# Other places for the opening loads, and the third pair of up-projection features split, summed and halved in another way

## The chip, the cores and the metric

The kernel runs on one core of one Trainium2 chip. The metric is the device time of one execution in microseconds (us); smaller is better. The core has a matrix engine (TensorE: PE in the profile, its weight loads PEld), VectorE (DVE), ScalarE (ACT), GpSimd (POOL) and SyncE (SP), which here issues the DMAs. All engines run their own instruction stream in order and wait for each other by semaphores.

## The reference, cut to what matters

One layer of an encoder for 1024 prompt rows and 64 sample rows of 1024 values. All is float32.

```python
z = einsum('btd,de->bte', x, w_in)            # one projection; columns: q_f k_f v_f f_lg u_g v_g q_s k_s v_s
log_f = log_sigmoid(f_lg + b_f)               # forget gates: 6 columns
o_f = fox_block(q_f, c, k_f, v_f)             # c = cumsum(log_f); softmax attention with forgetting
o_s = sb_block(q_s, k_s, v_s)                 # stick-breaking attention
o_g = sgu_mix(u, v, w_s, b_s)                 # spatial gating in chunks of 128
mix = rmsnorm_per_head(concat(o_f, o_g, o_s)) * g_mix @ w_out
x1 = layer_norm(ALPHA * x + mix)
y  = layer_norm(ALPHA * x1 + square(relu(x1 @ w_up)) @ w_down)
```

`w_up` has 4096 columns, here called features.

## The kernel before, in words

**Precision.** TensorE multiplies a fast 32-bit format (fp32r). So each operand is split into a high part (a ScalarE copy into fp32r) and a low part (`lo_sub`, L98: source minus high part, on VectorE or GpSimd), and each product is three matmuls: high by high, high by low, low by high (`PASSES`, a pair being the part of the rows and the part of the weights).

**Opening.** Row tile t of x (128 rows by 1024) is loaded by `x_load` (L312), transposed on TensorE in eight 128 by 128 blocks (`xtp`, L321) and split into `xT`. The weights of the first head pair stand in one tile `wkvfox` with 262 columns: 128 of K, 128 of V and 6 of the forget gates. `load_w` loads such columns in two groups g of four 128-row blocks each (`raw`, L337), ScalarE makes the high part (L338), and the low part is made on GpSimd for g = 0 and on VectorE for g = 1 (for the gates on GpSimd both). `load_kv` (L888) calls it for K, then loads row tile 1, then V, then the gates. A row tile's product with these weights is `kvfox` (L362), 24 matmuls per tile, group 0 of the weights first. Tiles of x are `row` buffers (seven places); K's raw weights have two `raw` places.

**Order.** Most of the program is written as generators whose steps are interleaved, and a scheduler with a model of time then fixes each engine's order. A change in one place can so move instructions far behind it. Two stretches are kept by `in_order`: every engine there runs as the code is written.

**Mix.** The output projection per row tile (`mx`, L251) takes the transposed heads `oTb`; LayerNorm of a tile, its store, and the transposes for the next tile and for the up-projection (`x_steps`) run between.

**Up-projection.** `w_up` is taken in 16 pairs of 128 features (p = 0 to 15), by a fast product scheme of seven half-size products instead of eight (`PROD`): operands 0, 1 and 3 are blocks of the weights, held in `wa[:, 0]`, `wa[:, 1]`, `wa[:, 2]`; operands 2, 4, 5 and 6 are sums of blocks, held in `ws`. Product 0 takes operand 0, product 1 operand 1, product 2 operand 5, product 3 operand 4. Each product is 12 matmuls for each of two groups of tokens (`Chain` s = 0 of 288 columns and s = 1 of 256). `prep(p)` splits the three blocks (`split` L1232: high on ScalarE, low on GpSimd), then `summed` makes the four sums in place in the raw tile `wr` (`w_sums`, L1241 to L1245, VectorE), `high` copies them to fp32r (L1514, ScalarE, in two halves) and `low` subtracts (VectorE, one instruction of 2048 columns). The first two sums overwrite the feature block f1, the last two f0; so the first waits for the split that reads f1's second half (operand 3), which is the third of the three. For p = 2 this stands inside the stretch kept by `in_order`, between the products of p = 1; from p = 2 on TensorE takes each product for both token groups.

**Down-projection.** It follows in the same manner; it isn't touched.

Of the kernel before, what the change touches and what calls it, by code (L numbers as in the profile page):

```python
# [12 lines left out]
F32 = mybir.dt.float32  # L13
# [7 lines left out]
P = 128  # L21
PASSES = ((0, 0), (0, 1), (1, 0))
D = 1024
# [14 lines left out]
OFF_QF, OFF_KF, OFF_VF, OFF_FL = 0, 384, 768, 1152  # L38
# [4 lines left out]
ROWS = 7  # L43
# [13 lines left out]
def _build(nc, tc, a, es):  # L57
    def trows(t):
        return P if t < NB else TS
# [7 lines left out]
    w_in = a["w_in"].rearrange("l d e -> (l d) e").rearrange("(k p) e -> p k e", p=P)  # L67
# [7 lines left out]
    def xrows(t):  # L75
        return x_p[t * P:(t + 1) * P, :] if t < NB else x_s
# [20 lines left out]
    def lo_sub(eng, out, src, hi):  # L97
        eng.tensor_tensor(out, src, hi.bitcast(F32), op=ALU.subtract)  # L98
# [187 lines left out]
    sp = p12.enter_context(tc.tile_pool(name="sp", bufs=1, side="left"))  # L286
# [3 lines left out]
    with ExitStack() as p1:  # L290
# [16 lines left out]

        xT = [big.tile([P, 4, 2 * TT], F32R, name=f"xT{i}", tag="xw") for i in range(2)]

        def x_load(t):  # L310
            xr = sp.tile([P, D], F32, name=f"xr{t}", tag="row", bufs=ROWS)
            nc.sync.dma_start(xr[0:trows(t), :], xrows(t))  # L312
            return xr

# [12 lines left out]
        def xh(k, h, c0, n):  # L327
            return xT[k // 4][:, k % 4, h * LO + c0:h * LO + c0 + n]

        def load_w(dst, c0, col, n, tag="raw", dve=()):  # L330
            for g in range(2):
                hi = dst[:, 4 * g:4 * g + 4, 0, c0:c0 + n]
                lo = dst[:, 4 * g:4 * g + 4, 1, c0:c0 + n]
                rt = sp.tile([P, 4, P if n == P else n], F32, name=f"raw{col}_{g}", tag=tag,
                             bufs={"raw": 2, "row": ROWS, "ft": 4}[tag])
                raw = rt[:, :, 0:n]
                nc.sync.dma_start(raw, w_in[:, 4 * g:4 * g + 4, col:col + n])  # L337
                nc.scalar.activation(hi, raw, AF.Copy)  # L338
                lo_sub(nc.vector if g in dve else nc.gpsimd, lo, raw, hi)

# [536 lines left out]
        for fox, hp in ((True, 2), (True, 1), (True, 0), (False, 0), (False, 1), (False, 2)):  # L877
            first = not pairs
# [4 lines left out]
                off=(OFF_QF, OFF_KF, OFF_VF) if fox else (OFF_QS, OFF_KS, OFF_VS),  # L883
# [4 lines left out]
        def load_kv(st):  # L888
            dve = (1,) if st["quick"] else ()
            w = st["wkv"] = sp.tile([P, KT, 2, 262], F32R, name=f"wkv{st['nm']}", tag="wkv", bufs=1)  # L890
            load_w(w, 0, st["off"][1] + st["hp"] * P, P, dve=dve)
            if st["first"]:
                xrs[1] = x_load(1)
                load_w(w, P, st["off"][2] + st["hp"] * P, P, "row", dve=dve)
                load_w(w, 2 * P, OFF_FL, 6, "ft")
            else:
                load_w(w, P, st["off"][2] + st["hp"] * P, P, dve=dve)

# [176 lines left out]
        xrs = {}  # L1075
# [18 lines left out]
        while f_live or a_live:  # L1094
# [11 lines left out]
            if go_a:  # L1106
# [5 lines left out]
                try:  # L1112
                    c = next(A)
# [8 lines left out]
            elif f_live:  # L1122
                try:
                    c = next(F)
# [27 lines left out]
    xr = rp.tile([P, 4096], F32, name="xr", tag="ws")  # L1152
# [78 lines left out]
    def split(hi, lo, raw, eng):  # L1231
        nc.scalar.activation(hi, raw, AF.Copy)  # L1232
        lo_sub(eng, lo, raw, hi)


    def w_sums(f0, f1, part=(0, 1)):

        a, b = slice(0, 4), slice(4, 8)
        tt = nc.vector.tensor_tensor
        if 0 in part:  # L1240
            tt(f1[:, b], f1[:, a], f1[:, b], op=ALU.add)  # L1241
            tt(f1[:, a], f0[:, a], f1[:, a], op=ALU.subtract)
        if 1 in part:
            tt(f0[:, a], f1[:, b], f0[:, a], op=ALU.subtract)  # L1244
            tt(f0[:, b], f0[:, b], f0[:, a], op=ALU.subtract)  # L1245
# [100 lines left out]
    for i in range(MIXED, NT):  # L1346
        t = ORD[i]
# [24 lines left out]
    def first_chain(s):  # L1372

        sn = [sp.tile([P, 288], F32, name=f"sn0_{s}_{q}", tag="gl", bufs=3) for q in range(2 + s)]

        class Some:
            def __getitem__(self, at):
                return sn[at[1]][:, at[2]]
        if s == 0:
            h = []  # L1380

            def hh(a, b):

                if not h:
                    h.append(sp.tile([P, 7, NS[s]], F32, name=f"h7_{s}", tag="wq", bufs=1))
                    h.append(sp.tile([P, 1, NS[s]], F32, name=f"h1_{s}", tag="raw", bufs=2))
                if a == 4:
                    return h[1]
                return h[0][:, a:b] if b <= 4 else h[0][:, a - 1:b - 1]
            return Chain(0, s, Some(), hh, ((2, 4), (4, 5), (5, 6)))  # L1390
        h44 = [yrow[t].rearrange("p (b c) -> p b c", b=4) for t in (3, 7)]
        return Chain(0, s, Some(), lambda a, b: h44[a // 4][:, a % 4:(b - 1) % 4 + 1], ((2, 4), (4, 6)))
# [87 lines left out]
    with p3:  # L1480
        def up_load(p):
            r = lp.tile([P, KT, 256], F32, name=f"wr{p}", tag="wr")

            for c in ((0, P), (P, 256)) if p == 2 else ((0, 256),):
                nc.sync.dma_start(r[:, :, c[0]:c[1]], w_up[:, :, p * 256 + c[0]:p * 256 + c[1]])
            return r[:, :, 0:P], r[:, :, P:256], r

        def prep(p, rest=True, raw=None):
            raw = raw or up_load(p)
            pool = rp if p % 2 else lp  # L1490
            wa = pool.tile([P, 3, 2, 4, P], F32R, name=f"wa{p}", tag="wa")
            f0, f1 = raw[0:2]
            a, b = slice(0, 4), slice(4, 8)
            for o, src in ((0, f0[:, a]), (1, f0[:, b]), (2, f1[:, b])):
                split(wa[:, o, 0], wa[:, o, 1], src, nc.gpsimd)
            whole = len(raw) == 3
            parts = ((slice(0, 256), raw[2]),) if whole else ((slice(0, P), f0), (slice(P, 256), f1))

            wsp = []

            def summed(part=(0, 1)):
                w_sums(f0, f1, part)
                if 1 not in part:
                    return
                ws = pool.tile([P, 2, KT, 256], F32R, name=f"ws{p}", tag="ws")
                wsp.append(ws)
                wops[p].update({2: ws[:, :, b, 0:P], 4: ws[:, :, b, P:256],
                                5: ws[:, :, a, 0:P], 6: ws[:, :, a, P:256]})

            def high():  # L1510
                ws = wsp[0]
                for q in (a, b) if whole else (slice(0, 8),):
                    for c, src in parts:
                        nc.scalar.activation(ws[:, 0, q, c], src[:, q], AF.Copy)  # L1514

            def low():
                ws = wsp[0]
                for c, src in parts:
                    lo_sub(nc.vector, ws[:, 1, :, c], src, ws[:, 0, :, c])

            wops[p] = {0: wa[:, 0], 1: wa[:, 1], 3: wa[:, 2]}
            if rest:
                summed()
                high()
                low()
            return summed, high, low
# [7 lines left out]
        t = ORD[-1]  # L1534
        next(x2)
        with in_order(border):
# [3 lines left out]
            c0 = first_chain(0)  # L1540
# [46 lines left out]
        with in_order(border):  # L1587
            raw = up_load(2)
# [115 lines left out]
    with ExitStack() as p3:  # L1704
# [229 lines left out]
        for c in range(NC - 1):  # L1934
            for part in range(2):
                g = 2 * c + part
# [39 lines left out]
        c = NC - 1  # L1976
# [21 lines left out]
        g = 2 * c  # L1998
# [135 lines left out]
```

## Time and profile before

| what | value |
|---|---|
| time, median of 3 runs | 1394.98 us (1391.84, 1394.98, 1395.25) |
| the profiled execution's own time | 1389.83 us |
| its span, first to last instruction | 1388.1 us |
| mean granted TensorE clock | 0.988 |
| TensorE busy | 1322.0 us, 95% |
| VectorE, ScalarE, GpSimd busy | 998.1, 719.1, 612.3 us |
| bytes moved by DMA | 185.64 MB |

How to read it: the span of the profiled execution lies 1.7 us below its own time, and that lies 2.0 to 5.4 us below the three timed runs, so runs of this program differ by about 0.3% among themselves. A row of the timeline gives start, duration, engine, line, operation, what it writes and reads, the count of merged instructions, and in brackets the idle time of the engine before it with what ended that. The clock is a column of the table by stretches: 1.00 is full speed. At the very start no clock event is on record before 17.3 us, so the column shows 1.00 there whatever the clock was.

### The profile page before, as it was taken

What the parts mean: (1) busy time and instruction counts of PE and PEld (TensorE: products, weight loads), DVE (VectorE), ACT (ScalarE), POOL (GpSimd) and SP (SyncE); (2) the same over time, 40 slices, a digit from 0 to 9 for tenths busy, and PEclk for the clock granted to TensorE, in tenths of its full rate; (3) what the DMA queues carried; (4) which work ended last, traced back from release to release, by engine and by line L of the source; (5) the groups of instructions that cost most, each with busy time, mean ns of one, the idle gap of its engine ahead of it and who ended that gap; (6) DMA issues with size and microseconds to landing.
All of it is one profiled execution on the core that took longest, in us unless ns stands there. A gap on an engine that the chain in (4) does not pass through costs nothing.

```text
span 1388.1 us, 24324 instructions
## 1 busy us (share of the span) xinstructions
PE 1322.0 (95%) x8827; PEld 1203.3 (87%) x8827; DVE 998.1 (72%) x1795; ACT 719.1 (52%) x1561; POOL 612.3 (44%) x667
## 2 busy tenths in 40 slices
PE   7999999999898998999999999999998999999996
PEld 7899989999888997877899999999986788887874
DVE  4577666576788379779866878767677677768677
ACT  4367566566556366334523222222266676767665
POOL 3231231256665446756412212212167675565547
PEclk9999999999999999999999999999999999999999
DMA  7445474231403247532234344344468334334333
GB/s 221 111 123 152 154 212 116 68 78 43 103 13 74 62 153 250 169 107 76 77 114 143 124 163 141 119 169 141 159 217 291 119 142 167 130 129 158 109 126 129
DMA packets 159088, 185.64 MB, mean 134 GB/s; under 512 B 27756, under 2 KB 117164, under 8 KB 158968
## 3 DMA queue, kind: packets, MB, share of 16 engines
q1 hardware_dynamic: 158968, 184.08, 41.7%
q8 instruction: 70, 1.15, 0.3%
q14 instruction: 50, 0.41, 0.1%
HBM read 117.65 MB, written 60.10 MB: 128 GB/s over the span
## 4 chain that ended last, share of the span: by engine, by line
PE 52%; DVE 15%; DMA 10%; ACT 9%; POOL 9%; issue 5%; SPq 0%; ACTq 0%; DVEq 0%; POOLq 0%
PE zA L1294 9%; PE zD L1294 6%; PE kvsb L362 5%; PE kvfox L362 4%; PE mx L251 4%; POOL wd L98 3%; PE zC L1294 3%; PE zB L1294 3%; PE A L1756 3%; DMA rd<-w_down 3%; POOL rd L1426 2%; DVE snsb L545 2%; DMA rwo<-w_out 2%; DMA awa<-h_dr 2%; DMA raw<-w_in 1%
## 5 line engine op out<-in xcount | busy, mean ns | idle before, releaser
L98 POOL TENSOR_TENSOR wa<-wr,wa 128x512 fp32r<-128x512 f32 x42 | 64.7, 1568 | 224.5 <-ACT wa L1232 224.5
L98 POOL TENSOR_TENSOR wd<-rd,wd 128x512 fp32r<-128x512 f32 x77 | 100.8, 1321 | 109.3 <-ACT wd L1232 109.1
L251 PE MATMUL mx<-xT,oTb 128*128 128x512 f32 (+1 forms) x416 | 104.4, 402 | 1.0 <-DVE oTb L98 1.0
L1294 PE MATMUL zA<-xo,ws 128*128 128x288 f32 (+1 forms) x720 | 98.6, 291 | 3.1 <-DVE ws L98 3.1
L1294 PE MATMUL zD<-xo,ws 128*128 128x288 f32 (+1 forms) x720 | 97.6, 289 | 2.6 <-DVE hh L1308 1.4
L1294 PEld LDWEIGHTS zA<-xo,ws 128*128 128x128 f32 x720 | 94.8, 191 | 3.3 <-DVE ws L98 3.3
L1294 PEld LDWEIGHTS zD<-xo,ws 128*128 128x128 f32 x720 | 93.5, 189 | 3.3 <-DVE hh L1308 1.9
L251 PEld LDWEIGHTS mx<-xT,oTb 128*128 128x128 f32 (+1 forms) x416 | 75.6, 187 | 19.5 <-DVE oTb L98 1.9
L1426 POOL TENSOR_TENSOR rd<-rd 128x512 f32<-128x512 f32 x56 | 79.5, 1419 | 29.4 <-DVE b L98 27.1
L547 POOL TENSOR_TENSOR sgsb<-sgsb,snsb 128x127 f32<-128x127 f32 (+7 forms) x48 | 58.5, 1219 | 75.7 <-DVE snsb L545 72.1
L362 PE MATMUL kvfox<-wkvfox,xT 128*128 128x256 f32 (+3 forms) x624 | 90.5, 293 | 1.1 <-ACT wkvfox L338 0.5
L362 PE MATMUL kvsb<-wkvsb,xT 128*128 128x256 f32 (+1 forms) x624 | 88.5, 287 | 0.0
L1232 ACT ACTIVATE wd<-rd 128x512 fp32r<-128x512 f32 x105 | 63.4, 623 | 47.3 <-POOL rd L1426 22.9
L1756 PE MATMUL A<-wd,wd 128*128 128x512 f32 x312 | 83.5, 396 | 3.2 <-DVE acc L1723 2.3
L362 PEld LDWEIGHTS kvfox<-wkvfox,xT 128*128 128x128 f32 (+1 forms) x624 | 81.6, 193 | 2.5 <-ACT wkvfox L338 0.9
L545 DVE TENSOR_TENSOR_SCAN snsb<-snsb,one 128x128 f32<-128x128 f32 (+7 forms) x48 | 72.5, 1514 | 15.3 <-ACT snsb L544 14.7
L362 PEld LDWEIGHTS kvsb<-wkvsb,xT 128*128 128x128 f32 (+1 forms) x624 | 79.5, 187 | 0.2
L1305 ACT ACTIVATE sn<-zA 128x256 f32<-128x256 f32 (+1 forms) x80 | 31.0, 390 | 93.2 <-PE zA L1294 82.2
L1756 PEld LDWEIGHTS A<-wd,wd 128*128 128x128 f32 x312 | 58.0, 188 | 19.6 <-DVE acc L1723 4.0
L1756 PE MATMUL A<-wd,h4a 128*128 128x512 f32 x240 | 64.7, 394 | 1.4 <-POOL wd L98 0.8
L1514 ACT ACTIVATE ws<-wr 128x1024 fp32r<-128x1024 f32 x28 | 29.2, 1056 | 58.4 <-DVE wr L1244 57.9
L1756 PEld LDWEIGHTS A<-wd,h4a 128*128 128x128 f32 x240 | 44.8, 188 | 13.0 <-POOL wd L98 1.2
(548 smaller groups left out, 3748.9 us busy)
## 6 DMA issues: line engine op xcount, KB each, us to landing
h_dr<-hh SPq DMA_DIRECT2D x30, 512.0 KB, 3.2
rd<-w_down SPq DMA_DIRECT2D x30, 512.0 KB, 4.4
wr<-w_up SPq DMA_DIRECT2D x13, 1024.0 KB, 5.5
hr<-h_dr SPq DMA_DIRECT2D x31, 384.0 KB, 4.5
h_dr<-hh SPq DMA_DIRECT2D x30, 384.0 KB, 3.8
raw<-w_in SPq DMA_DIRECT2D x44, 256.0 KB, 3.5
wo_dr<-swo SPq DMA_DIRECT2D x32, 256.0 KB, 2.5
xT<-wo_dr SPq DMA_DIRECT2D x8, 1024.0 KB, 8.0
```

Of the source, the lines that this page charges most:

```text
L98: eng.tensor_tensor(out, src, hi.bitcast(F32), op=ALU.subtract)
L251: nc.tensor.matmul(acc[0:m], oT[:, k, hx, 0:m], wo[k // 4][hw][:, k % 4, cs], start=(i == 0), stop=(i == len(seq) - 1))
L362: nc.tensor.matmul(acc[0:n, c0:c0 + n1 - n0], xT[k // 4][:, k % 4, c:c + n], wt[:, k, hw, n0:n1], start=(i == 0), stop=(i == len(seq) - 1))
L545: nc.vector.tensor_tensor_scan(g[:, 0:n][:, ::-1], g[:, 0:n][:, ::-1], one.broadcast_to([P, n]), 1.0, op0=ALU.mult, op1=ALU.bypass)
L547: nc.gpsimd.tensor_tensor(s[:, 0:n - 1], s[:, 0:n - 1], g[:, 1:n], op=ALU.mult)
L1232: nc.scalar.activation(hi, raw, AF.Copy)
L1294: nc.tensor.matmul(z, w[:, hw, k], xop(s, bo, hx)[:, k, :], start=(new and k == 0 and j == 0), stop=(k == 3 and j == 2), skip_group_check= ...
L1305: nc.scalar.activation(c, z, AF.Copy)
L1426: eng.tensor_tensor(r[:, o], r[:, x], r[:, y], op=ALU.subtract)
L1514: nc.scalar.activation(ws[:, 0, q, c], src[:, q], AF.Copy)
L1756: nc.tensor.matmul(z, h[:, hx, q, o], wset[self.c % 2][q][:, hw, wb], start=((n in (0, 3) or n == 1 and self.c == 0) and q == 0 and j == 0 ...
```

## The change

Three edits. **Opening:** the two loads of the gate columns are issued by ScalarE's queue at the start, ahead of everything else that ScalarE does but its table load; V's weights are loaded ahead of row tile 1 and in the order g = 1, g = 0; the buffer places are reserved so that later tiles keep theirs. **Up, p = 2 alone:** the three blocks are split in reverse order (operand 3, 1, 0), operand 3's low part on VectorE instead of GpSimd. **Up, p = 2 alone:** the low parts of the four sums are made in two halves (the halves that `high` already has).

```diff
-        def x_load(t):
-            xr = sp.tile([P, D], F32, name=f"xr{t}", tag="row", bufs=ROWS)
+        def x_place(t):
+            return sp.tile([P, D], F32, name=f"xr{t}", tag="row", bufs=ROWS)
+
+        def x_load(t, xr=None):
+            xr = x_place(t) if xr is None else xr
             nc.sync.dma_start(xr[0:trows(t), :], xrows(t))
             return xr
...
-        def load_w(dst, c0, col, n, tag="raw", dve=()):
-            for g in range(2):
+        def load_w(dst, c0, col, n, tag="raw", dve=(), landed=None, order=(0, 1)):
+            for g in order:
...
-                rt = sp.tile([P, 4, P if n == P else n], F32, name=f"raw{col}_{g}", tag=tag,
-                             bufs={"raw": 2, "row": ROWS, "ft": 4}[tag])
-                raw = rt[:, :, 0:n]
-                nc.sync.dma_start(raw, w_in[:, 4 * g:4 * g + 4, col:col + n])
+                if landed:
+                    raw = landed[g]
+                else:
+                    rt = sp.tile([P, 4, P if n == P else n], F32, name=f"raw{col}_{g}", tag=tag,
+                                 bufs={"raw": 2, "row": ROWS, "ft": 4}[tag])
+                    raw = rt[:, :, 0:n]
+                    nc.sync.dma_start(raw, w_in[:, 4 * g:4 * g + 4, col:col + n])
...
+            if st["first"]:
+
+                gates = []
+                for g in range(2):
+                    sp.tile([P, 512], F32, name=f"at_raw{g}", tag="raw", bufs=2)
+                for g in range(2):
+                    gates.append(sp.tile([P, 4, 6], F32, name=f"rawf_{g}", tag="ft", bufs=4))
+                    nc.scalar.dma_start(gates[g], w_in[:, 4 * g:4 * g + 4, OFF_FL:OFF_FL + 6])
             load_w(w, 0, st["off"][1] + st["hp"] * P, P, dve=dve)
             if st["first"]:
-                xrs[1] = x_load(1)
-                load_w(w, P, st["off"][2] + st["hp"] * P, P, "row", dve=dve)
-                load_w(w, 2 * P, OFF_FL, 6, "ft")
+                xrs[1] = x_place(1)
+                load_w(w, P, st["off"][2] + st["hp"] * P, P, "row", dve=dve, order=(1, 0))
+                x_load(1, xrs[1])
+                load_w(w, 2 * P, OFF_FL, 6, landed=gates)
...
-            for o, src in ((0, f0[:, a]), (1, f0[:, b]), (2, f1[:, b])):
-                split(wa[:, o, 0], wa[:, o, 1], src, nc.gpsimd)
+            blocks = ((0, f0[:, a]), (1, f0[:, b]), (2, f1[:, b]))
+
+            for o, src in blocks[::-1] if p == 2 else blocks:
+                split(wa[:, o, 0], wa[:, o, 1], src, nc.vector if p == 2 and o == 2 else nc.gpsimd)
...
-                for c, src in parts:
-                    lo_sub(nc.vector, ws[:, 1, :, c], src, ws[:, 0, :, c])
+                for q in (a, b) if p == 2 else (slice(0, 8),):
+                    for c, src in parts:
+                        lo_sub(nc.vector, ws[:, 1, q, c], src[:, q], ws[:, 0, q, c])
```

**What moves in the opening.** SP's queue from the program's start, before (`xr` is a row tile of x, `raw_0` and `raw_1` of 128 columns are the groups of K, V and later q, of 6 columns the gates):

```order
L312 DMA xr_117<-x_prompt 128x1024
L337 DMA raw_0_120<-w_in 128x4x128
L337 DMA raw_1_124<-w_in 128x4x128
L312 DMA xr_128<-x_prompt 128x1024
L337 DMA raw_0_130<-w_in 128x4x128
L337 DMA raw_1_134<-w_in 128x4x128
L337 DMA raw_0_138<-w_in 128x4x6
L337 DMA raw_1_142<-w_in 128x4x6
L312 DMA xr_146<-x_prompt 128x1024
```

and the same queue after the change (its line numbers are those of the changed file):

```order
L315 DMA xr_117<-x_prompt 128x1024
L343 DMA raw_0_126<-w_in 128x4x128
L343 DMA raw_1_130<-w_in 128x4x128
L343 DMA raw_1_135<-w_in 128x4x128
L343 DMA raw_0_139<-w_in 128x4x128
L315 DMA xr_134<-x_prompt 128x1024
L315 DMA xr_148<-x_prompt 128x1024
```

Row tile 1 (`xr_128`, now `xr_134`) is the sixth transfer instead of the fourth, and the gates have left the queue.

TensorE from its first instruction on, before (`xtp` are transposes of row tiles 0 and 1, `kvfox` the products):

```order
L321 MATMUL xtp_0_163<-ident,xr_117 128x128 x4
L321 MATMUL xtp_1_170<-ident,xr_117 128x128 x4
L321 MATMUL xtp_0_211<-ident,xr_128 128x128 x4
L321 MATMUL xtp_1_218<-ident,xr_128 128x128 x4
L362 MATMUL kvfox_0_177<-wkvfox_119,xT_109 128x262
```

and after:

```order
L324 MATMUL xtp_0_165<-ident,xr_117 128x128 x4
L324 MATMUL xtp_1_172<-ident,xr_117 128x128 x4
L368 MATMUL kvfox_0_179<-wkvfox_119,xT_109 128x262
L324 MATMUL xtp_0_213<-ident,xr_134 128x128 x4
L324 MATMUL xtp_1_220<-ident,xr_134 128x128 x4
L368 MATMUL kvfox_0_179<-wkvfox_119,xT_109 128x262 x11
```

One product matmul now stands ahead of row tile 1's transposes; the other 47 of the first two tiles still stand behind them.

ScalarE from its first instruction on, after the change (`rawf` are the gates; before, the gates' two splits stood behind those of K and V):

```order
L1089 ACT_TABLE_LOAD
L904 DMA rawf_122<-w_in 128x4x6
L904 DMA rawf_124<-w_in 128x4x6
L344 ACTIVATE wkvfox_119<-rawf_122 128x4x6
L344 ACTIVATE wkvfox_119<-raw_0_126 128x4x128
L326 ACTIVATE xT_109<-xtp_0_165 128x4x128
L344 ACTIVATE wkvfox_119<-rawf_124 128x4x6
L344 ACTIVATE wkvfox_119<-raw_1_130 128x4x128
L326 ACTIVATE xT_110<-xtp_1_172 128x4x128
L344 ACTIVATE wkvfox_119<-raw_1_135 128x4x128
L344 ACTIVATE wkvfox_119<-raw_0_139 128x4x128
```

The first split waits for the gates' landing, and all of ScalarE's work stands behind it.

**What moves at p = 2.** VectorE there, before (`wr` the raw weights under the sums, `hh`, `sn`, `z` the results of the chains of p = 1 and 2):

```order
L1308 TENSOR_TENSOR hh_1_9250<-zD_1_9300,sn_1_9249 128x256
L1241 TENSOR_TENSOR wr_9149<-wr_9149 128x4x128
L1242 TENSOR_TENSOR wr_9149<-wr_9149 128x4x128
L1244 TENSOR_TENSOR wr_9149<-wr_9149 128x4x128
L1310 TENSOR_TENSOR hh_0_9394<-zB_0_9425,sn_0_9393 128x288
L1245 TENSOR_TENSOR wr_9149<-wr_9149 128x4x128
L1312 TENSOR_TENSOR hh_1_9250<-sn_1_9249,zC_1_9341 128x256
L98 TENSOR_TENSOR ws_9338<-wr_9149,ws_9338 128x2048
```

and after:

```order
L1323 TENSOR_TENSOR hh_1_9252<-zD_1_9302,sn_1_9251 128x256
L98 TENSOR_TENSOR wa_9329<-wr_9151,wa_9329 128x512
L1256 TENSOR_TENSOR wr_9151<-wr_9151 128x4x128
L1257 TENSOR_TENSOR wr_9151<-wr_9151 128x4x128
L1259 TENSOR_TENSOR wr_9151<-wr_9151 128x4x128
L1260 TENSOR_TENSOR wr_9151<-wr_9151 128x4x128
L1327 TENSOR_TENSOR hh_1_9252<-sn_1_9251,zC_1_9343 128x256
L98 TENSOR_TENSOR ws_9340<-wr_9151,ws_9340 128x1024 x2
```

VectorE makes operand 3's low part itself, ahead of the sums; GpSimd has two low parts left, operand 1's and then operand 0's. In the mix, about 130 us ahead of this, the scheduler has also placed TensorE's transposes, VectorE's and GpSimd's steps of LayerNorm and SP's stores a little otherwise, though no code there is changed; the counts of instructions there are the same.

## The prediction

> **What bounds the kernel now.** I read the page first: TensorE is busy 95% of the span, so only its 66 us of idle time, and its stretches at half clock, can be won.
>
> ```profile
> span 1388.1 us, 24324 instructions
> PE 1322.0 (95%) x8827; PEld 1203.3 (87%) x8827; DVE 998.1 (72%) x1795; ACT 719.1 (52%) x1561; POOL 612.3 (44%) x667
> ```
>
> The second view is the list of TensorE's waits; the up-projection has one entry of size, and the table by stretches shows what follows it (columns: stretch, its length, busy time of PE, PEld, DVE, ACT, POOL, granted clock, DMA share, GB/s).
>
> ```profile
> PE zA L1294 <- DVE ws L98: 3.1, 1, 3.1
> 728.00:731.00 3.00, 0.03 (x1) 0.00 (x0) 2.26 (x2) 0.71 (x1) 0.00 (x0) 0.95 0.00 0
> 731.00:734.00 3.00, 2.91 (x12) 2.91 (x13) 2.86 (x7) 0.38 (x1) 0.00 (x0) 0.50 0.54 156
> 760.00:780.00 20.00, 20.00 (x160) 20.00 (x159) 16.51 (x24) 5.24 (x10) 5.00 (x3) 1.00 0.29 91
> ```
>
> TensorE stands for 3 us, then runs 3 us at half clock; 30 us later it is never idle. So p = 2 is alone in this. The timeline there gives the cause.
>
> ```profile
> 719.32 1.66 ACT L1232 ACTIVATE wa<-wr 128x512 fp32r<-128x512 f32 x3
> 720.02 3.80 POOL L98 TENSOR_TENSOR wa<-wr,wa 128x512 fp32r<-128x512 f32 x3 [25.17 <-ACT wa L1232]
> 721.68 3.19 PE L1294 MATMUL zA<-xo,wa 128*128 128x288 f32 x24
> 723.85 0.69 DVE L1241 TENSOR_TENSOR wr<-wr 128x512 f32<-128x512 f32 x1 [3.97 <-POOL wa L98]
> 724.70 3.19 PE L1294 MATMUL zB<-xo,wa 128*128 128x288 f32 x24
> 726.03 1.06 ACT L1514 ACTIVATE ws<-wr 128x1024 fp32r<-128x1024 f32 x1 [2.09 <-DVE wr L1244]
> 727.73 0.30 PE L1294 MATMUL zA<-xo,ws 128*128 128x288 f32 x1
> 728.74 2.29 DVE L98 TENSOR_TENSOR ws<-wr,ws 128x2048 fp32r<-128x2048 f32 x1 [0.79 <-ACT ws L1514]
> 731.09 4.51 PE L1294 MATMUL zA<-xo,ws 128*128 128x288 f32 x23 [3.06 <-DVE ws L98]
> 735.43 3.19 PE L1294 MATMUL zD<-xo,ws 128*128 128x288 f32 x24
> ```
>
> Read upwards: product 2 (727.73) waits for the sums' low parts, these for their high parts, those for the sums, and VectorE stood 3.97 us for GpSimd's third low part, operand 3's. The products start at 721.68, 724.70, 727.73: 3.02 apart. The next starts 7.70 after product 2, so 4.67 us are lost: 3.06 of wait, the rest half clock.
>
> **The change at p = 2.** VectorE is free at 719.88 and ScalarE's first high part stands by 720.02, where GpSimd took it; VectorE now makes operand 3's low part there and the first two sums behind it, each at the 0.69 of its sum row: 720.7, then 722.1. That wait of 3.97 goes. GpSimd has two parts left, now operand 1's, then operand 0's, and product 0 needs operand 0: its first matmul is high by high, its second needs the low part. Where one stood ahead of it, there are now a copy and two.
>
> ```profile
> L98 POOL TENSOR_TENSOR wa<-wr,wa x42: 1286/1465/2447, 720.0 to 982.8; 128x512 fp32r<-128x512 f32 x42
> 700.50 2.36 DVE L98 TENSOR_TENSOR ws<-y,ws 128x1024 fp32r<-128x1024 f32 x2 [0.85 <-ACT ws L1514]
> ```
>
> (Least, median and greatest ns of one in the first row.) GpSimd starts one high copy later, 1.66/3 = 0.55 after 720.02, at 720.6. Two parts take 2.57 at the least (the three in 3.80 ran so, with VectorE idle) and 2.93 at the median, which I take since VectorE now works beside it: done at 723.5. Product 0's second matmul stood ready at 721.8: **a new wait of 1.3 to 1.7 us, taken as 1.7**; at the greatest, 2.45 each, it would be 3.6. Behind that waiting matmul all of TensorE is queued.
>
> What comes next: the last two sums overwrite f0, which GpSimd reads until 723.5, so they end at 724.9 (2 x 0.69); the halves of `high` at 725.9 and 727.0 (1.06 each); the low halves, 1.18 each by the row of 700.50, at 727.2 and 728.4 with some 0.1 between engines. Product 2 now stands two products behind 723.5, at about 729.4: both halves are there with 1 us left. The halving thus costs nothing and matters little: unhalved, 727.0 + 2.3 = 729.3 would be just in time. Its extra instruction on VectorE lies beside TensorE's products. Net: 1.7 - 4.67 = **-3.0 us**, if the clock stays up.
>
> Whether it does hangs on the wait's size. Two other waits, with the stretch in which each lies and the stretch behind it:
>
> ```profile
> 379.03 0.60 PE L640 MATMUL otpsb<-ident,osbsb 128*128 128x128 f32 x2 [1.73 <-ACT osbsb L632]
> 375.70:379.10 3.40, 1.67 (x16) 1.55 (x15) 2.47 (x5) 2.63 (x7) 1.76 (x2) 1.00 0.78 219
> 379.20:382.50 3.30, 3.30 (x17) 3.30 (x17) 2.75 (x9) 1.85 (x7) 2.27 (x8) 0.50 0.36 87
> 302.14 0.38 PE L619 MATMUL osb<-pthsb,vpsb 128*128 128x256 f32 x1 [2.02 <-ACT osbsb L632]
> 300.60:304.00 3.40, 1.86 (x16) 1.86 (x17) 3.13 (x8) 2.39 (x8) 1.94 (x4) 1.00 0.52 131
> 304.10:307.40 3.30, 3.30 (x31) 3.30 (x30) 2.39 (x3) 2.22 (x9) 3.05 (x5) 1.00 0.21 60
> ```
>
> 1.67 busy of 3.40 was followed by half clock, 1.86 was not. A lone wait of 1.7 leaves 1.7 busy if it falls wholly into one such stretch, and more if it is cut by a border: the clock more likely stays. If it goes, half of 3.4 us is lost, 1.7.
>
> The Trainium skill ("TensorE: Matmul & The Clock Gate", section "Why this matters for your kernels") asks only for no idle gaps over about 3 us; by it the new wait never costs the clock and the term is -3.0 at any phase. The trace differs: the 1.73 us ahead of 379.03 were followed by 0.50.
>
> **The change in the opening.**
>
> ```profile
> 2.80 4.21 SPq L337 DMA_DIRECT2D raw<-w_in  x4
> 7.05 3.20 SPq L312 DMA_DIRECT2D xr<-x_prompt  x4
> 8.99 1.97 PE L321 MATMUL xtp<-ident,xr 128*128 128x128 f32 x8 [2.62 <-DMA xr<-x_prompt]
> 9.70 0.63 ACT L338 ACTIVATE wkvfox<-raw 128x512 fp32r<-128x512 f32 x1 [0.92 <-DMA raw<-w_in]
> 10.71 0.85 ACT L338 ACTIVATE wkvfox<-raw 128x512 fp32r<-128x512 f32 x3
> 11.50 8.95 PE L362 MATMUL kvfox<-wkvfox,xT 128*128 128x262 f32 x48 [0.54 <-ACT wkvfox L338]
> 12.38 7.85 PEld L362 LDWEIGHTS kvfox<-wkvfox,xT 128*128 128x128 f32 x46 [0.38 <-POOL wkvfox L98]
> 4.00:8.50 4.50, 1.94 (x8) 1.57 (x8) 0.87 (x2) 1.95 (x4) 1.27 (x1) 1.00 1.07 310
> 8.50:10.00 1.50, 1.01 (x5) 1.02 (x6) 1.12 (x2) 0.58 (x2) 0.00 (x0) 1.00 0.70 98
> 20.00:40.00 20.00, 20.00 (x170) 19.95 (x169) 9.77 (x20) 8.34 (x19) 6.11 (x15) 1.00 0.51 135
> raw<-w_in SPq DMA_DIRECT2D x2, 12.0 KB, 6.5
> bf<-b_f SPq DMA_DIRECT2D x2, 3.0 KB, 8.7
> ```
>
> TensorE runs without a gap from 12.38 on, and is full in 20 to 40, so what is won at 12.38 stays. Removed from SP's queue: two gate loads. Moved: row tile 1 behind V, so that the six large transfers up to both row tiles, K and V (two of 512 KB, four of 256 KB, 2.0 MB) are the same as before in another order. The last of them, then V's second group, was through before ScalarE's run of three splits at 10.71, say at 10.4. Now the last is row tile 1, at 10.4; with the gates' tiny rows ahead of it instead of behind, up to 1.0 later. Its eight transposes (1.97) stand ahead of 47 of the 48 product matmuls, which so run from 12.4 to 13.3 instead of 12.38: 0 to +0.9. V's splits, which gave TensorE its 0.54 and 0.38 of wait, are then done ahead of need. From the other side: 8.5 to 10.0 moved 98 GB/s where 310 had been moved. If the gates made that lull (their four neighbours took SP 4.21 us to issue) and it goes, some 1.0 of it is saved, and the half clock at which TensorE starts can end one stretch earlier, 1.7: -2.7. I take **0**, the row nearest to what must land ahead of the products.
>
> The Trainium skill ("DMA: Bandwidth & Descriptors", section "Issuing engines are not separate DMA queues") says that transfers issued by different engines run on the same 16 DMA engines and interleave, so only sequencer time is saved; by it the -2.7 falls away and 0 to +0.9 stays. No run here shows it yet.
>
> **Elsewhere.** The mix is reordered, in equal counts. Its largest wait now, and two stretches beside it:
>
> ```profile
> 676.91 0.63 PE L1168 MATMUL xtc<-ident,y 128*128 128x128 f32 x4 [1.19 <-DVE xr L1188]
> 540.00:560.00 20.00, 16.76 (x93) 14.20 (x92) 18.32 (x32) 10.10 (x23) 15.52 (x14) 0.83 0.79 265
> 560.00:580.00 20.00, 20.00 (x105) 16.53 (x104) 14.37 (x31) 6.48 (x13) 12.32 (x14) 1.00 0.37 111
> ```
>
> There is about that much to win, and as much to lose: 0, between -2 and +2 by these rows.
>
> **Sum.** -3.0 + 0 + 0 on the profiled execution's 1389.83 is 1386.8. The three timed runs lie 2.0, 5.2 and 5.4 above the profiled one, 4.2 in the mean: **1391.0 us**, 0.22% under it. About 0.3%, 4.2 us, is what a measurement can tell here.
>
> **Rivals.**
> - *The new wait costs the clock* (its place: product 0; it decides from 1.7 us on). Another 1.7 or so: -1.5, 1392.5. For: GpSimd's greatest, 2447. Against: borders of the stretches cut a lone wait.
> - *The opening gains*, -2.7: -5.7 in all, 1388.3. For: the lull of 98 GB/s. Against: the bytes ahead of row tile 1 don't change.
> - *The gates hold ScalarE*: its first split now waits for them, and all its work stands behind. They took 6.5 us from issue to landing, b_f's small rows 8.7. If they land only at 10.8, about where ScalarE first touches them now (10.71), its work up to V's last split comes behind that: K's two splits and the two copies of transposes (1.95 for four in 4.0 to 8.5), V's two (0.63 each), the gates' two (0.11 each, from 0.85 for three less 0.63), 3.4 in all. The first product matmul then runs at 14.2, the transposes behind it end at 16.2, and the products start 3.8 after 12.38: +0.8 in all, 1394.8. Against: the queues are empty when they are issued.
> - *Slower: the reordered mix gets one stretch like 540 to 560*: 3.1 of idle time and 3.4 lost to the clock at 0.83, 6.5, so +3.5, 1397.5. It decides once waits leave TensorE busy under half of a 3.4 us stretch. Against: TensorE is full in 560 to 580, and the counts are equal.
> - *It doesn't do what it says*, product 2 still waiting: the sums would have to slip by over 1 us behind 723.5. I leave it within the first rival.
>
> **How the numbers follow.** Forecast 0.46 (of it 0.12 ends under -0.3%, by a win in the mix or the opening's half); new wait with clock 0.14; opening gains 0.20; gates hold ScalarE 0.10; mix slower 0.10 (0.01 of it within 0.3%). Faster by over 0.3%: 0.12 + 0.20 = 0.32. Slower: 0.09. Same: 0.59. The range: from 1386.0, the opening's case less 2.3 for the mix and the scatter of runs, to 1396.5, short of the slower rival.
>
> **What would show it.** Right: TensorE's wait for VectorE at product 2 is gone, a wait of 1.3 to 1.7 for GpSimd stands at the second matmul of product 0, the clock is full at 730; row tile 1's transposes end at 12.4 to 13.3; the mix's waits add up as before. Wrong: a half clock behind product 0; ScalarE's first copy later than 7; products from under 11.5 on; a new stretch at half clock between 557 and 690.

## The result and the profile after

The change takes **1384.26 us** (median of 4 runs, 1382.49 to 1385.90), the kernel before 1394.6 (4 runs, 1391.84 to 1395.25): ratio 0.9937, 95% interval 0.992 to 0.9955. A repetition gave 1384.3 against 1391.27 (26 runs of before), 0.9946 (0.9928 to 0.9965). By the two ratios it is 7.5 to 8.8 us faster, and it lies below the forecast range, which began at 1386.0. The repeated runs of before reach from 1387 to 1395, so three of the four at hand, near 1395, lay high. One of the 12 runs of e4 below took 5880.26 us; it counts as slow and is in neither that run's median nor its ratio, and why it was slow is not known.

The page and TensorE's waits after:

```profile
span 1384.0 us, 24332 instructions
PE 1320.5 (95%) x8827; PEld 1202.0 (87%) x8827; DVE 998.8 (72%) x1797; ACT 719.5 (52%) x1561; POOL 611.3 (44%) x666
```

```profile
PE xtp L324 <- DMA xr<-x_prompt: 4.4, 1, 4.4
PE Sfox L567 <- DMA qdfox<-qdfox: 3.1, 1, 3.1
PE zA L1309 <- POOL wa L98: 1.6, 1, 1.6
```

TensorE's wait for VectorE at p = 2 is gone and a wait of 1.6 for GpSimd has come, as forecast. The wait for row tiles is 4.4 instead of 7.0: that for row tile 1 is gone, but TensorE now waits 2.51 for V's weights at nearly the same place (8.88 below). One for a copy of q (`qdfox`) is new among the longest. The timeline at p = 2:

```profile
719.64 0.69 DVE L98 TENSOR_TENSOR wa<-wr,wa 128x512 fp32r<-128x512 f32 x1
720.21 2.96 POOL L98 TENSOR_TENSOR wa<-wr,wa 128x512 fp32r<-128x512 f32 x2 [25.67 <-DMA h_dr<-hh]
720.37 1.67 DVE L1256 TENSOR_TENSOR wr<-wr 128x512 f32<-128x512 f32 x1
721.35 0.29 PE L1309 MATMUL zA<-xo,wa 128*128 128x288 f32 x1
722.08 1.63 DVE L1257 TENSOR_TENSOR wr<-wr 128x512 f32<-128x512 f32 x1
723.22 3.16 PE L1309 MATMUL zA<-xo,wa 128*128 128x288 f32 x23 [1.58 <-POOL wa L98]
723.82 0.69 DVE L1259 TENSOR_TENSOR wr<-wr 128x512 f32<-128x512 f32 x1
724.55 2.01 ACT L1531 ACTIVATE ws<-wr 128x1024 fp32r<-128x1024 f32 x2 [3.89 <-DVE wr L1259]
725.64 2.36 DVE L98 TENSOR_TENSOR ws<-wr,ws 128x1024 fp32r<-128x1024 f32 x2
729.24 3.19 PE L1309 MATMUL zA<-xo,ws 128*128 128x288 f32 x24
732.27 3.19 PE L1309 MATMUL zD<-xo,ws 128*128 128x288 f32 x24
```

Product 0's second matmul waits 1.58 for GpSimd's two parts; product 2 starts at 729.24, 3.03 behind product 1, with its weights done at 728.0. The opening after:

```profile
4.54 0.22 ACT L344 ACTIVATE wkvfox<-rawf 128x24 fp32r<-128x24 f32 x1 [2.46 <-DMA rawf<-w_in]
8.88 0.59 PE L368 MATMUL kvfox<-wkvfox,xT 128*128 128x262 f32 x1 [2.51 <-ACT wkvfox L344]
9.32 1.97 PE L324 MATMUL xtp<-ident,xr 128*128 128x128 f32 x8
10.94 6.95 PE L368 MATMUL kvfox<-wkvfox,xT 128*128 128x262 f32 x47
```

```profile
8.50:10.00 1.50, 1.12 (x4) 0.97 (x5) 0.78 (x2) 0.32 (x1) 1.10 (x1) 1.00 1.00 410
50.00:55.00 5.00, 1.89 (x15) 1.36 (x14) 3.79 (x11) 2.66 (x8) 1.27 (x1) 0.90 0.68 114
55.00:60.00 5.00, 5.00 (x24) 5.00 (x25) 3.39 (x5) 0.09 (x1) 0.00 (x0) 0.50 0.85 182
720.00:740.00 20.00, 18.42 (x146) 18.21 (x146) 13.53 (x21) 6.50 (x13) 6.74 (x5) 1.00 0.37 123
```

Where 98 GB/s had moved, 410 do. The gates landed at 4.51 and 5.79; the 47 products run from 10.94 instead of 12.38, where 46 of 48 did, and take 6.95. They are shorter because the first clock event on record is at 13.09 instead of 17.32: in both traces these matmuls follow each other every 0.22 us ahead of that event and every 0.12 behind it. When it comes is in part a matter of the execution: in two more profiles of the old opening it is at 14.48 and 15.79, in six more of the new at 11.92 to 13.93. At 50 to 60 this profile gives the gain back: a wait of 3.1 and then half clock. At 720 to 740 the clock stays full.

One pair of profiles doesn't make a ledger here, because half-clock stretches fall elsewhere in each execution. So the table takes all profiles of this study. Each column is the time between the starts of the same two TensorE instructions, named by their times in before; where a row is of several profiles, it is their mean.

| stretch (us in before) | 4-30 | 30-75 | 75-540 | 540-690 (mix) | 712-760 (p = 2) |
|---|---|---|---|---|---|
| before | 25.8 | 44.9 | 465.0 | 150.0 | 48.0 |
| before, second profile (e0) | 26.6 | 46.9 | 464.4 | 150.9 | 48.2 |
| after | 23.2 | 47.5 | 465.3 | 149.2 | 45.1 |
| old opening, 3 profiles (before, e0, e2) | 26.3 | 45.9 | 464.2 | 150.6 | |
| new opening, 7 profiles (after, e1, e3 to e7) | 23.3 | 46.2 | 464.5 | 149.1 | |
| old p = 2, 5 profiles (before, e0, e1, e4, e5) | | | | | 47.7 |
| new p = 2, 4 profiles (after, e2, e3, e7) | | | | | 45.1 |

The opening is worth -3.0, of which +0.3 and +0.3 are given back up to 540; the mix -1.5; p = 2 -2.6. Together -6.5, inside the interval of the repetition (-4.9 to -10.0 on 1391.3). In the one pair, before and after, the 2.6 won at 4 to 30 is all lost again at 30 to 75.

### The profile page after: what moved, and what is told of

Its sections match the earlier page's. It is cut to its first block, busy times and chain, and to the rows that moved or that the text cites. A ratio compares the mean times of both kernels' runs of the same rounds, so it can differ in the third digit from the quotient of the medians.

```text
span 1384.0 us, 24332 instructions
## 1 busy us (share of the span) xinstructions
PE 1320.5 (95%) x8827; PEld 1202.0 (87%) x8827; DVE 998.8 (72%) x1797; ACT 719.5 (52%) x1561; POOL 611.3 (44%) x666
## 4 chain that ended last, share of the span: by engine, by line
PE 66%; DVE 11%; DMA 8%; ACT 6%; POOL 4%; issue 4%; SPq 0%; ACTq 0%; DVEq 0%; POOLq 0%
PE A L1774 10%; PE zA L1309 9%; PE zD L1309 6%; PE mx L251 5%; PE D L1774 5%; PE kvsb L368 5%; PE kvfox L368 4%; PE zB L1309 3%; PE zC L1309 3%; DMA rwo<-w_out 3%; PE B L1774 2%; DVE snsb L551 1%; PE qsb L509 1%; PE qfox L509 1%; PE Ssb L567 1%
## 5 line engine op out<-in xcount | busy, mean ns | idle before, releaser
L1441 POOL TENSOR_TENSOR rd<-rd 128x512 f32<-128x512 f32 x56 | 79.3, 1416 | 28.9 <-DVE b L98 26.6
L1247 ACT ACTIVATE wd<-rd 128x512 fp32r<-128x512 f32 x105 | 63.6, 624 | 46.4 <-POOL rd L1441 23.3
```

What stands on the lines that cost most here:

```text
L1441: eng.tensor_tensor(r[:, o], r[:, x], r[:, y], op=ALU.subtract)
```

## The experiments

**e0: before against itself.**

> The kernel before, unchanged, against itself: a control, and a second profile of it. Theory A (the profiled execution of before had fewer half-clock stretches behind waits than the timed runs, which lie 2.0 to 5.4 us above it): the ratio is 1.000 within 0.002, the times lie between 1390 and 1395, and the second profile has half-clock stretches at other places, with a sum of lost time up to 5 us larger than the 13 us or so of the first. Theory B (the scatter is something else, the profiled time being low by a fixed amount): the half-clock stretches stand at the same waits, and the profiled time is again some 4 us below the timed ones.

Measured: ratio 1.0006 (0.9991 to 1.0021), 12 runs from 1387.8 to 1397.1; the profiled execution took 1397.07 where the first took 1389.83. Theory A holds, with wider bounds than the 1390 to 1395 it gave: two executions of one program differ by 7.2 us. The wait of 3.06 at p = 2 is the same; other half-clock stretches (at 59, 1025 and 1335 us) stand in only one of the two.

**e1: the opening alone.** The hunks of the diff on `x_load`, `load_w` and `load_kv`, without those on `wa` and `low`.

> The opening edit alone. Theory A (the edits are independent; the opening wins 2.5 us by row tile 1's earlier landing, some of it is given back at 54 us where TensorE waits for the second copy of q by DMA, and the mix is 0.8 better): TensorE's product behind 20 us starts 2.5 earlier, the offset behind 60 us is -1.6 or so where the clock stays up there and +0.8 where it drops, and the time is 2 to 4 us less: ratio 0.997 to 0.9985. Theory B (the opening is the larger part of the whole 8.8 us, by fewer half-clock stretches all along the attention): ratio 0.995 to 0.9965, with fewer half-clock stretches than the control between 55 and 560 us.

Measured: 1385.71 (9 runs), ratio **0.9958** (0.9943 to 0.9973). That is larger than theory A had it, but not by theory B's means: between 55 and 560 us this profile has no fewer half-clock stretches than the control. The stretch 4-30 takes 23.5 (26.6 in the control, 25.8 in the first profile of before), the mix 149.5 (150.9 in the control). The order of the mix moves with the opening alone; the p = 2 edits alone leave it as it was.

**e2: p = 2 alone.** The hunks on `wa` and `low`.

> The two edits at p = 2 alone. Theory A: TensorE waits 1.6 to 1.8 us for GpSimd at product 0, nothing at product 2, no half clock there: 2.8 us less, ratio 0.998, and everything ahead of 720 us as in the control. Theory B (the removed half-clock stretch there is worth more than the profile showed, since the wait of 3.06 costs it at every phase, and sometimes 6.8 us of it): ratio 0.9955 to 0.997.

Measured: 1389.36 (12 runs), ratio **0.9988** (0.9972 to 1.0003). The interval takes in 1, so the time alone doesn't show the gain; its middle is nearer to theory A's 0.998. By its profile 712 to 760 takes 45.1, and the wait is the forecast one:

```profile
722.52 0.29 PE L1294 MATMUL zA<-xo,wa 128*128 128x288 f32 x1
724.39 3.16 PE L1294 MATMUL zA<-xo,wa 128*128 128x288 f32 x23 [1.58 <-POOL wa L98]
```

By the profile it is theory A. How much the old wait cost is a matter of the moment, though. The same wait in e1, where p = 2 is unchanged:

```profile
728.57 3.16 PE L1309 MATMUL zA<-xo,ws 128*128 128x288 f32 x23 [3.06 <-DVE ws L98]
```

```profile
726.00:729.00 3.00, 0.43 (x3) 0.43 (x4) 2.74 (x3) 0.23 (x2) 0.00 (x0) 1.00 0.00 0
729.00:732.00 3.00, 3.00 (x26) 3.00 (x26) 2.73 (x5) 0.77 (x2) 0.00 (x0) 1.00 0.72 207
```

and in the control:

```profile
731.00:734.50 3.50, 0.44 (x4) 0.28 (x3) 2.71 (x3) 0.84 (x1) 0.00 (x0) 1.00 0.00 0
734.70:738.00 3.30, 3.30 (x17) 3.30 (x16) 2.68 (x5) 0.72 (x2) 0.00 (x0) 0.50 0.81 230
```

A wait of 3.06 or 3.07 was followed by full clock in e1, e4 and e8, by 3.4 us of half clock in before, e0 and e9, and 6.8 us of it stand around the wait in e5. So the edit saves 1.5, the difference of the two waits, and by the stretch 712 to 760 about 1.4 to 1.6 more against before and e0 and 2.6 more against e5.

**e3: the whole change again.**

> The whole change, unchanged, once more: ratio 0.9937 within its interval, 0.992 to 0.9955. Theory A: the ratio is the product of those of the opening alone and of p = 2 alone within 0.001, and this profile's half-clock stretches stand at other places than 54, 194, 402, 443 and 552 us. Theory B (the two edits help each other): the whole is better than the product by 0.002 or more.

Measured: 0.9946 (0.9928 to 0.9965); the product of the two parts is 0.9958 x 0.9988 = 0.9946. The parts add up. The second half of theory A fails: four of the five half-clock stretches stand at the same places again (53, 401, 442 and 551); only that at 194 is missing, and ones at 227, 381 and 1015 have come.

**e4: the gates early, the rest of the opening as before.** Against e1:

```
-                xrs[1] = x_place(1)
-                load_w(w, P, ..., "row", dve=dve, order=(1, 0))
-                x_load(1, xrs[1])
+                xrs[1] = x_load(1)
+                load_w(w, P, ..., "row", dve=dve)
```

> Half of the opening edit: the gates' two loads by ScalarE's queue at the start, but row tile 1 ahead of V and V's groups in the old order. No edit at p = 2. Theory A (the gates' rows of 24 bytes, standing between the large loads, made the lull of 73 to 201 GB/s at 8.5 to 10.0, and their going made the gain): 8.5 to 10.0 moves 400 GB/s, the long run of products starts at 10.6 to 11.2 instead of 12.38, and the ratio is that of the whole opening edit, 0.9958 within 0.0015. Theory B (V ahead of row tile 1 made the gain): the products start at 11.8 or later and the ratio is 0.998 to 1.000.

Measured: 1385.68 (11 runs), ratio **0.9966** (0.9949 to 0.9982).

```profile
10.47 7.24 PE L368 MATMUL kvfox<-wkvfox,xT 128*128 128x262 f32 x46 [0.28 <-POOL wkvfox L98]
```

```profile
8.50:10.00 1.50, 1.50 (x8) 1.39 (x6) 0.58 (x2) 1.50 (x4) 0.86 (x1) 1.00 1.04 422
```

The lull is gone and the products start at 10.47, 0.5 earlier even than in the whole change. This run alone would speak for theory A.

**e5: V ahead of row tile 1, the gates by SP behind it.** Against e1:

```
-                    nc.scalar.dma_start(gates[g], w_in[...])
...
                 x_load(1, xrs[1])
+                for g in range(2):
+                    nc.sync.dma_start(gates[g], w_in[...])
```

> The other half of the opening edit: V (second group first) ahead of row tile 1, and the gates' two loads by SP's queue behind it. No edit at p = 2. Theory A: the gates land at 10.5 to 11 as before, the first product matmul needs them and stands ahead of row tile 1's transposes, so that the long run of products starts at 12.4 to 13.6, and the ratio at the start is 0.999 to 1.001 (0.998 with the mix, which is reordered here too). Theory B: the long run starts at 10.6 to 11.2 as in the whole opening edit, ratio 0.9958 within 0.0015.

Measured: 1386.47 (12 runs), ratio **0.9971** (0.9954 to 0.9987).

```profile
9.39 0.42 ACT L344 ACTIVATE wkvfox<-rawf 128x24 fp32r<-128x24 f32 x2 [0.88 <-DMA rawf<-w_in]
10.79 7.39 PE L368 MATMUL kvfox<-wkvfox,xT 128*128 128x262 f32 x48
```

Against theory A: the gates stand in the same place of SP's queue as before, land at 9.4 to 9.6 instead of 10.6 to 10.8, and the products start at 10.79. So either half of the edit brings nearly the whole gain without the other (the intervals of e1, e4 and e5 overlap). The small rows by themselves don't make the lull: 8.5 to 10.0 moves 367 GB/s in e5.

**What the landings say.** A trace has 16 completion updates for each load, read here as one for each of the 16 DMA engines; which engine sent one isn't told. The eighth of them (the middle) and the last, in us:

```
            K, second group   row tile 1     V, the later group   gates (last)
before      5.70   7.64       7.27   8.94     8.77   10.42         10.84
e0          5.83   7.21       7.29   8.55     8.81   10.07         10.50
e2          5.69   7.87       7.22   9.18     8.75   10.60         11.04
after       6.40   6.54       8.97   9.28     7.71    8.02          5.79
e4          6.25   6.48       7.48   7.71     8.86    9.14          5.73
e5          5.52   6.34       8.58   9.13     7.25    7.86          9.57
```

In the old opening the last update of K's second group comes 1.4 to 2.2 behind the middle one (this is called the lag below), and 1.2 to 2.0 behind in the loads from there to the gates. It isn't always one engine that is late: of V's later group, two of the 16 updates come over 0.5 behind the middle in before, four in e0, one in e2. In the seven changed openings the lag is 0.1 to 0.8. The landing of 10.42 on which the forecast rested was that of the late ones; the middle one landed at 8.77.

The lull goes with a second thing. The middle engines have the gates done by 9.27, and the next load, row tile 2, came late from SP. Its issue in before:

```profile
7.05 1.78 SPq L312 DMA_DIRECT2D xr<-x_prompt  x1
```

So it took until 8.83; in e0 until 8.46, in e2 until 9.01. In e5, where it also stands behind the gates, it took 0.64 and ended at 6.46. That this slow issue and the late engines have one cause is not shown.

**Which landing the products start behind.** In the old order GpSimd releases them. Before and in e4:

```profile
10.41 2.11 POOL L98 TENSOR_TENSOR wkvfox<-raw,wkvfox 128x512 fp32r<-128x512 f32 x3 [3.28 <-ACT wkvfox L338]
9.14 1.27 POOL L98 TENSOR_TENSOR wkvfox<-raw,wkvfox 128x512 fp32r<-128x512 f32 x1 [0.99 <-ACT wkvfox L344]
```

Before, the gates' low parts stand behind that of V's first group, and the first of them ended at 12.32, just ahead of the products; in e4 they are done by then. V's first group landed at 9.67 in before and at 8.41 in e4. From its landing to the products' start it is 2.70 or 2.71 in before, e0 and e2, and 2.06 in e4, e8 and e9. So of the 1.91 by which e4 starts earlier, 0.65 is GpSimd's order and 1.26 the landing. Where V stands ahead of row tile 1 (after, e1, e3, e5, e6, e7), the products start 1.66 to 1.68 behind row tile 1's landing instead.

**e8 and e9: what causes the late landings.** Against e4, one line each:

```
-                    nc.scalar.dma_start(gates[g], w_in[...])
+                    nc.gpsimd.memset(gates[g], 0.0)        # e8
+                    nc.sync.dma_start(gates[g], w_in[...]) # e9
```

> The opening of the kernel before with the gates' two loads left out (GpSimd writes zeros there, so the forget gates see only their bias); row tile 1 ahead of V, no edit at p = 2. What is told apart is why, in three profiles of the old opening, one DMA engine's share of K's second group landed 1.4 to 2.2 us behind the middle one and stayed so far behind through row tile 1 and V, while it is 0.1 to 0.8 in the seven of the changed openings. Theory A (the gates' loads, issued by SP while the large ones run, cause the lag): without them the lag is under 0.5, row tile 1 lands by 7.5 and V's second group by 9.0, and the long run of products starts at 10.2 to 10.8. Theory B (the order row tile 1, V causes it): the lag stays at 1.3 to 2.2, and they start at 12 or so. This is one look at the profile; the time is not compared.

Measured: without any gate load the lag is still 1.6 at K's second group and 1.1 to 1.2 at row tile 1 and V (landed 8.46 and 9.99). So SP's issue of the gates isn't needed for a lag, which speaks against theory A, by this one profile. There is no lull, though: 8.5 to 10.0 moves 420 GB/s. By this profile the lull goes with the gates, and the lag doesn't need them. The products start at 11.29, between the two theories:

```profile
8.50 1.97 PE L324 MATMUL xtp<-ident,xr 128*128 128x128 f32 x8 [2.17 <-DMA xr<-x_prompt]
10.12 0.89 PE L368 MATMUL kvfox<-wkvfox,xT 128*128 128x262 f32 x2
11.29 7.35 PE L368 MATMUL kvfox<-wkvfox,xT 128*128 128x262 f32 x46 [0.28 <-POOL wkvfox L98]
```

So of the 1.9 from 12.38 (before) to 10.47 (e4), 1.1 is there in e8: 0.65 by GpSimd's order and 0.44 by V's first group, which landed at 9.23. The other 0.8 is its landing at 8.41 in e4, where the lag is 0.2 to 0.3.

> The opening with the gates issued early, but by SP's queue, right behind row tile 0 and ahead of K; row tile 1 ahead of V, no edit at p = 2. Theory A (it is the moment of the gates' issue that matters, not the queue): K is issued some 1.2 to 1.5 us later by SP, but the transfers stand in line anyway, so row tile 1 lands at 7.7 to 8.4, the lag is under 0.8, and the long run of products starts at 10.5 to 11.3. Theory B (another engine's queue is what helps): the lag is 1.3 to 2.2 again, row tile 1 lands at 9 or later and the products start at 12 or later. One look at the profile.

Measured: lag 1.0 at K's first group, 0.6 from its second on; row tile 1 landed at 8.76, and

```profile
8.80 1.97 PE L324 MATMUL xtp<-ident,xr 128*128 128x128 f32 x8 [2.44 <-DMA xr<-x_prompt]
11.57 6.96 PE L368 MATMUL kvfox<-wkvfox,xT 128*128 128x262 f32 x46 [0.28 <-POOL wkvfox L98]
```

That is between the two theories, with the lag from K's second group on as A has it. Early by SP's own queue wins 0.8 on 12.38 (0.65 of it GpSimd's order), by ScalarE's 1.9. e4 and e9 differ in that queue alone: in e9 K is issued 1.0 later (2.26 instead of 1.25), row tile 1 lands 1.05 later and the products start 1.1 later. So the issue did count, against theory A's "the transfers stand in line anyway".

What makes the lag is left open. In the six profiles in which ScalarE's queue issues the gates it is 0.1 to 0.4 at K's second group; in the six with SP's queue alone it is 0.6 to 2.2. But e5 issues the same first three loads at the same times as before and has 0.8 there, so the queue may not be all of it; with one profile each of e4, e5, e8 and e9, scatter between executions isn't ruled out.

**e6: operand 0 first on GpSimd.** Against the change:

```
-            for o, src in blocks[::-1] if p == 2 else blocks:
+            for o, src in (blocks[2], blocks[0], blocks[1]) if p == 2 else blocks:
```

> The whole change, with the blocks of p = 2 split in the order operand 3, 0, 1, so that GpSimd makes operand 0's low part first. Theory A (the wait of 1.58 at product 0 is GpSimd's second low part, and nothing stands behind it): the wait falls to under 0.2, product 1 and product 2 don't wait, and the stretch from 715 to 760 is 1.4 to 1.6 us shorter than with the change: ratio 0.9935. Theory B (operand 1 then comes too late, or the sums of f0 do): a wait of 0.5 to 1.5 at product 1 or 2, ratio 0.9945.

Measured: **1379.85** (6 runs), ratio **0.9924** (0.9901 to 0.9947); the fastest of all, though its interval overlaps that of the change. The profile is clear:

```profile
714.11 2.99 POOL L98 TENSOR_TENSOR wa<-wr,wa 128x512 fp32r<-128x512 f32 x2 [25.67 <-DMA h_dr<-hh]
715.25 3.36 PE L1309 MATMUL zA<-xo,wa 128*128 128x288 f32 x24
719.57 2.47 DVE L98 TENSOR_TENSOR ws<-wr,ws 128x1024 fp32r<-128x1024 f32 x2
721.47 3.19 PE L1309 MATMUL zA<-xo,ws 128*128 128x288 f32 x24
```

```profile
713.00:733.00 20.00, 20.00 (x161) 19.87 (x160) 13.57 (x20) 7.44 (x14) 6.78 (x5) 1.00 0.40 136
```

Products 0 to 2 follow without a gap, and 712 to 760 takes 43.5 instead of 45.1, in this one profile. That is theory A: the wait of 1.58 was the order on GpSimd, and nothing stands behind it. Here product 2 starts at 721.47, while the second low half ends only at 722.04, and doesn't wait.

**e7: no halving.** Against the change: `for q in (slice(0, 8),):`.

> The whole change without the halving: the low parts of the four sums of p = 2 in one instruction of 2048 columns again. Theory A (the earlier sums do it, the halving has next to no part): the low part ends 0.1 to 0.4 ahead of product 2 and TensorE waits there 0 to 0.3 us; the ratio is that of the change, 0.9946, within 0.001. Theory B (the halving is needed): product 2 waits 1 us or more, with a half clock behind it, ratio 0.996 to 0.997.

Measured: ratio 0.9946 (0.9925 to 0.9968), p = 2 as in the change (45.1).

```profile
724.70 2.29 DVE L98 TENSOR_TENSOR ws<-wr,ws 128x2048 fp32r<-128x2048 f32 x1 [1.02 <-ACT ws L1531]
727.35 3.19 PE L1309 MATMUL zA<-xo,ws 128*128 128x288 f32 x24
```

That is theory A: the one low part ends at 726.99, 0.36 ahead of product 2. In the change as it stands the halving does nothing. In e6, where product 2 started before the second half was done, it may matter; that wasn't run without it.

## Why the prediction was right and wrong, point by point

- **p = 2: right.** Forecast -3.0, between the two profiles -2.8, in the mean of the profiles -2.6. New wait forecast 1.3 to 1.7, measured 1.58; product 2 forecast to start with margin, it did; the halving worth nothing, so it was (e7). One duration was wrong and hidden: the first two sums took 1.67 and 1.63, not 0.69, and product 2 didn't wait for them. GpSimd's two parts took 2.96 where 2.93 was forecast, but as 1.29 and 1.71, not as twice the median.
- **The clock at p = 2: right for the new wait, too sure of the old.** The new wait cost no clock in any of four profiles. The working took the old dip of 1.6 as certain; e1, e4 and e8 show the old wait without it.
- **The opening, the step that failed.** The prediction took row tile 1, now the last of the six large transfers, to land at 10.4, where V's second group had landed, and put 0 into the sum. It landed at 9.28, and the products started at 10.94, 1.66 behind it, not 1.97. The 10.42 was the landing of late DMA engines, 1.65 behind the middle one. The argument from equal bytes held for the middle one (8.77 before, 8.97 after); what shrank is the lag, from 1.65 to 0.31. A sign of that was quoted: 98 GB/s in a stretch in which ScalarE waited for V. It was given to a rival at 0.20. That rival (*the opening gains*, -2.7: 1.0 on the landing, 1.7 on the clock) is what happened in size: -2.6 in the pair, 1.44 of it on the products' start and 1.1 on the clock, and -3.0 in the mean. The clock's part is in part luck, as the spread of the first clock event shows; e0 and e2, whose event came earlier than that of before, instead wait 2.01 and 1.05 for VectorE at 29.6 to 29.7, which no new opening does. The rival's condition, that the gates made the lull, fits e8 (no gates, no lull) and not e5 (gates by SP, no lull); and e8, without a lull, still starts only at 11.29. Why the engines are late stays open.
- **The rule that issuing engines share the DMA engines.** The Trainium skill ("DMA: Bandwidth & Descriptors", section "Issuing engines are not separate DMA queues") says that only sequencer time is saved by another issuing engine, and the text drew from it that -2.7 falls away. e5 agrees with the rule (all by SP's queue, products at 10.79) and not with what was drawn from it: here other places for the loads in the one queue bring the gain, and the rule says nothing of those.
- **The gates holding ScalarE:** didn't happen; its first split ran at 4.54 after a wait of 2.46 for the gates, ahead of K's landing at 5.53.
- **The mix: 0 forecast within -2 and +2, measured -1.5**, in a mean of 7 profiles against 3. The wait of 1.19 at 676.91 is gone from TensorE's list after. Half clock there is 6.8 us in all seven, and 6.8, 3.4 and 3.4 in the three old ones, so the gain isn't the clock's. What else the new order changes was not followed up, so most of this cause is open.
- **The base.** 4.2 us were added for the three timed runs; the 26 of the repetition have their median at 1391.27, not at 1394.0. By that, some 2.7 of the 6.7 by which the forecast lay above 1384.3 are the base; the rest is mostly the opening (2.4 net) and the mix (1.5).

## What to carry to other kernels

Look at all completion updates of a load and not at the last alone. Where the last comes well behind the middle one (1.65 here), the landing isn't set by the bytes, and time can be won without moving fewer of them. The GB/s of the stretch tell it only sometimes: 98 in before, 420 in e8, with a lag in both. Then find the engine that releases the waiting one and count from the landing to it: here that was 2.06, 2.70 or 1.66 in every profile, by what stood in line. Where one engine makes several operands, put the one that is needed first in front: it was worth 1.6 us here for one line, by the profile. And before believing a few microseconds in one profile, profile the unchanged kernel twice: here the two lay 7.2 apart.

## What the runs showed of the hardware that was not expected

- VectorE's sums of 128x512 took 1.67 and 1.63 while GpSimd ran beside them, 0.69 behind it; GpSimd's first part, begun ahead of them, took 1.29 and its second 1.71. The four profiles of this order (after, e2, e3, e7) agree within 0.01. The Trainium skill ("GPSIMD Engine Reference", section "1. Specifications") says that GpSimd shares its SBUF interfaces with VectorE, with contention where VectorE has two inputs from SBUF; the trace agrees.
- A wait of one and the same length, 3.06 to 3.07, came with 0, 3.4 or 6.8 us of half clock in different executions. The Trainium skill ("TensorE: Matmul & The Clock Gate", section "What's actually happening") says that the window in which the clock looks at activity runs freely and isn't reset by the kernel; the runs agree.
- One to five of the 16 completion updates of a load came 0.5 us or more behind the middle one from the third load on, in all three profiles of the old opening, the last of them 1.2 to 2.2 behind; in the one without gates it was 1.1 to 1.6. What made them late is not settled.
